# A fused mixer layer: the first two row pairs in eight plain products, and VectorE's SBUF pairs issued as scalar_tensor_tensor

## The chip, the cores and the metric

One NeuronCore of a Trainium2 chip runs the whole layer in one launch. The engines are PE (TensorE: matmuls and, through an identity matrix, transposes), DVE (VectorE), ACT (ScalarE), POOL (GpSimd) and SP, whose queue issues every DMA here. Each engine takes its instructions strictly in order and waits on semaphores for the others. The metric is device time in microseconds; each time below is the median of three runs or that of the one profiled execution.

## The reference, cut to what matters

```python
h = layer_norm(x, ln_emb_g, ln_emb_b)                    # x: 4096 rows x 1024
a_val, a_gate, a_z, b_u, b_v, b_z = split(h @ w_in, 6)   # six parts of 512 columns
y_a = silu(layer_norm(depthwise_conv31(a_val * sigmoid(a_gate)))) * silu(a_z)
y_b = gelu(b_u) * (w_s_lower_triangular @ layer_norm(gelu(b_v)) + b_s) * silu(b_z)
h = layer_norm(2**0.25 * h + concat(y_a, y_b) @ w_out)
h = h + sigmoid(h @ w_ple_gate + b_ple_gate) * (p @ w_ple)
```

Everything is float32.

## The kernel before, in words

The matrix work is five units of the same form, (4096 x 1024) times (1024 x 1024): `a_val|a_gate`, `b_u|b_v`, `b_z|a_z`, `w_out` and `w_ple_gate`. Below they are units A to E. A unit walks over 16 pairs of row blocks, 256 rows each. Within a pair both factors are cut into 2 x 2 blocks of 512 (256 rows are two blocks of 128), and the pair is computed in seven block products instead of eight: `group` forms products 1 to 7 of sums of blocks. `rows_left` makes the row sums s1 to s4 of a pair, `first_operands` and `combos` make the weight sums. A product is exact to float32 through a split: each factor is a high part (fp32r) and a low rest, and `product` issues three matmuls (high x high, high x low, low x high) for each of four k slices, so 12 matmuls of 128x128 by 512 columns a product, and 84 a pair.

The left factors are rows: loaded (`load_x`), normalised (`h_rows`: statistics on DVE, a power and a bias on POOL, scaling on ACT, then a multiply and an add by the embedding's gain and shift `eb`), turned by PE in groups of four transposes into one of two spare PSUM banks (tag "S"), copied by ACT (`zq`), split (`left`: high part by ACT, rest by DVE or POOL) and written to `qD` in DRAM for units B and C. `split_weight` makes the high part of a weight on ACT and the rest on DVE, by TENSOR_TENSOR on two SBUF operands. The rows of pair 1 are finished by DVE, those of later pairs by POOL.

Unit A starts from nothing: `load_first` loads four weight blocks, `first_operands` builds the sums W5, W6, W7, W4 in place and splits seven operands before pair 0. `open_banks` writes zeros by matmul into banks A and D, because `group` adds products onto copies that lie there. Later units get their weights from DRAM (`load_operands`, seven reads of 1 MB in the last pair of the unit before).

The convolution runs in the background on DVE, in chains of SCALAR_TENSOR_TENSOR (`conv`), with one SBUF operand and one PSUM accumulator each. Its two row buffers have the tag "ca"; nothing uses them until pair 3 of unit A has been written out. A scheduler arranges the instructions of each engine when the program is built, so the order of code is not the order on an engine; `tc.issue_after` keeps a piece of background work behind a given instruction.

Of the kernel before, what the change touches and what calls it, by code (L numbers as in the profile page):

```python
# [16 lines left out]
P = 128  # L17
# [47 lines left out]
def hybrid_layer_kernel(  # L65
# [51 lines left out]
    def flat(t):  # L117
        return t.rearrange("p k x -> p (k x)")
# [89 lines left out]

    def first_operands(W, stg):
        b11, b12, b22, b21 = (stg[ij] for ij in ((0, 0), (0, 1), (1, 1), (1, 0)))  # L210

        def sub(dst, a, b):
            for c in range(2):
                cs = slice(2 * c, 2 * c + 2)
                tt(dst[:, cs], a[:, cs], b[:, cs], op=SUB)
# [12 lines left out]

    def left(src, eng):
# [15 lines left out]
    def rows_left(L, rows, keep=None):  # L245
# [7 lines left out]
        def turn(n, j, half):  # L253
            tp = sbank("tp")
            for kk in range(4):
                k = 4 * half + kk
                nc.tensor.transpose(  # L257
                    out=tp[:, kk * P : (kk + 1) * P], in_=rows[:, j, k * P : (k + 1) * P],
                    identity=ident,
                )  # L260
            if keep is not None:
                act(zq[:, n], tp, ID)
            return quad(tp)
# [39 lines left out]
        yield  # L303

    def product(ps, n, L, W, start):
        ah, al = L[n]
        wh, wl = W[n]
# [6 lines left out]
    def open_banks():  # L316

        z = atile("zero")
        nc.gpsimd.memset(z.bitcast(F32), 0.0)
        for tag in ("A", "D"):  # L320
            nc.tensor.matmul(pbank(tag, "seed"), lhsT=z[:, 0, :], rhs=flat(z), start=True, stop=True)

    anchor = []

# [99 lines left out]
    def unit(u, L, W, next_left, next_first, body, conv_quota, lag=0):  # L424


        for p in range(NP):
# [9 lines left out]
            def between(i):  # L437
                bg_x.step(2 if lag else 1)
                if i >= lag:
                    bg.step(3 if lag else 2)  # L440
                bg_post.step(2)
                if last and u + 1 < 5:
                    bg_w.step(2 if i == 5 else 1)
                else:
                    bg_w.step(1)
                if i in (2, 3):
                    with tc.issue_after(anchor[0].ins):
                        bg_conv.step(conv_quota)
# [11 lines left out]
    X = {}  # L460

    def load_x(p):
        X[p] = big([P, 2, D], "xr")
        for j in (1, 0):
            dma(X[p][:, j], x[(2 * p + j) * P : (2 * p + j + 1) * P, :])

    def first_rows():

        r = X[0]
        for j in (1, 0):  # L470
            mv = mvtile(1)
            moments([r[:, j, 0:C], r[:, j, C:]], mv[:, 0, :])
            nb = scale_bias(mv)
            act(r[:, j], r[:, j], ID, scale=mv[:, 0, 1:2], bias=nb[:, 0:1])
            for half in (0, 1):
                v = r[:, j, half * C : (half + 1) * C]
                tt(v, v, eb[:, 0, half * C : (half + 1) * C], op=MUL)
                tt(v, v, eb[:, 1, half * C : (half + 1) * C], op=ADD)
            dma(hT[0][j], r[:, j])

    def h_rows(p, eng):

        r = X[p]
        mv = mvtile(2)
        for j in (1, 0):
            moments([r[:, j, 0:C], r[:, j, C:]], mv[:, j, :])
        yield
        nb = scale_bias(mv)
        for j in (1, 0):
            act(r[:, j], r[:, j], ID, scale=mv[:, j, 1:2], bias=nb[:, j : j + 1])  # L490
            eng.tensor_tensor(r[:, j], r[:, j], eb[:, 0], op=MUL)
            eng.tensor_tensor(r[:, j], r[:, j], eb[:, 1], op=ADD)
            dma(hT[p][j], r[:, j])
            yield
# [3 lines left out]
    eb = broadcast(erow, 2, "eb")  # L498
    stg = load_first()
    first_rows()  # L500
    open_banks()
    L = {}
    for _ in rows_left(L, X.pop(0), qD[0]):
        pass
    first_operands(W, stg)
    dma(cw_sb, cw)
# [3 lines left out]
    dma(bs_sb, bsv)  # L510
    load_x(1)
    for _ in h_rows(1, nc.vector):
        pass

    def left_a(p, L):
        return rows_left(L, X.pop(p), qD[p])

# [22 lines left out]
    def body_a(p, L, W, between):  # L540
        if p + 2 < NP:
            load_x(p + 2)
            bg_x.add(h_rows(p + 2, nc.gpsimd))
        if p == 3:
            bg_w.add(combos(1))
        c12, c22 = utile([P, C], "c12"), utile([P, C], "c22")
        pa, pd = group(L, W, None, c12, c22, between)
        for ps, c in ((pa, c12), (pd, c22)):
            act(c, c, AF.Sigmoid)
            tt(c, ps, c, op=MUL)  # L550
# [17 lines left out]
    act(wsx[:, 0], wsf, ID)  # L568
    tt(wsx[:, 1], wsf, wsx[:, 0].bitcast(F32), op=SUB)
    V = {}  # L570
# [17 lines left out]
    def body_b(p, L, W, between):  # L588
# [6 lines left out]
        def norm_v(j, v):  # L595
# [5 lines left out]
            act(v, v, ID, scale=mv[:, 0, 1:2], bias=nb[:, 0:1])  # L601
            tt(v, v, sgb[0][:, 0], op=MUL)
            tt(v, v, sgb[1][:, 0], op=ADD)
            act(V["h"][:, i], v, ID)
# [92 lines left out]
    def left_y(p, L):  # L697
        return rows_left(L, Y.pop(p))

# [61 lines left out]
    def left_z(p, L):  # L761
        return rows_left(L, Z[p])

# [125 lines left out]
```

## Time and profile before

| | us |
|---|---|
| median of three runs (lowest, highest) | 1899.16 (1896.24, 1899.81) |
| the profiled execution's own time | 1898.2 |
| its span, first to last instruction | 1896.5 |
| PE busy in the span | 1804.0 (95%) |
| DVE busy | 1413.6 (75%) |
| POOL busy | 1269.9 (67%) |
| ACT busy | 892.4 (47%) |

PE's busy time counts matmuls that overlap, so it says where PE stands still rather than how fast it goes. Of the 92 us in which PE is idle, 33 lie in the first 60 us; most of the rest lies where one unit ends and the next begins.

### The profile page before, as it was taken

The page shows a single profiled execution, that of the slowest core. Times are in us where ns is not written, and L with a number is a line of the kernel's source. Part 1 is how long each engine was busy: PE and PEld are TensorE (multiplying, and loading weights), DVE is VectorE, ACT ScalarE, POOL GpSimd, SP SyncE. Part 2 cuts the span into 40 slices and gives each one's busy share as a digit, 9 for nine tenths or more (in the row PEclk, how much of TensorE's full clock was granted, in tenths as well). Part 3 has the DMA queues.
Part 4 walks back from the last instruction along what each step waited for, and adds up shares of the span by engine and source line. Part 5 has one row for each costly group of instructions (what it writes and reads, how often), then busy time and mean ns, then how long its engine had stood idle before and what let it go on. Part 6 is the DMA issues. An engine that isn't in the chain of part 4 may idle for free. (4 is left out here: it accounts for less than half of the span.)

```text
span 1896.5 us, 24392 instructions
## 1 busy us (share of the span) xinstructions
PE 1804.0 (95%) x8322; PEld 1470.9 (78%) x8322; DVE 1413.6 (75%) x2176; ACT 892.4 (47%) x1438; POOL 1269.9 (67%) x1015
## 2 busy tenths in 40 slices
PE   4799999999999999999999899999999999999999
PEld 3687788877788887788888677787887787888887
DVE  8637877797787778978787998887558856665654
ACT  4655555565455555544444634445555422332222
POOL 2878987458777676588668568757676856655541
PEclk9899999999999999999999889999999999999999
DMA  6579776586734445898666758745555322222311
GB/s 239 195 236 359 248 235 206 194 287 211 239 124 147 139 142 173 302 358 298 211 198 227 272 186 284 242 150 191 197 189 220 119 95 78 89 90 95 100 54 52
DMA packets 184940, 363.62 MB, mean 192 GB/s; under 512 B 49648, under 2 KB 74224, under 8 KB 177136
## 3 DMA queue, kind: packets, MB, share of 16 engines
q1 hardware_dynamic: 184816, 362.07, 55.3%
q8 instruction: 66, 1.08, 0.2%
q14 instruction: 58, 0.48, 0.1%
HBM read 211.02 MB, written 150.99 MB: 191 GB/s over the span
## 5 line engine op out<-in xcount | busy, mean ns | idle before, releaser
L232 POOL TENSOR_TENSOR alo<-s,ahi 128x512 fp32r<-128x512 f32 x192 | 262.8, 1382 | 260.7 <-ACT ahi L231 252.9
L312 PE MATMUL pb<-whi,ahi 128*128 128x512 f32 x960 | 385.9, 402 | 18.3 <-ACT pa L330 5.2
L313 PE MATMUL pb<-wlo,ahi 128*128 128x512 f32 x960 | 378.4, 394 | 1.6 <-DVE wlo L173 1.6
L314 PE MATMUL pb<-whi,alo 128*128 128x512 f32 x960 | 378.4, 394 | 0.1
L312 PE MATMUL pe<-whi,ahi 128*128 128x512 f32 x640 | 258.9, 405 | 19.6 <-ACT ahi L231 8.5
L314 PE MATMUL pe<-whi,alo 128*128 128x512 f32 x640 | 256.6, 401 | 2.1 <-POOL alo L232 2.1
L313 PE MATMUL pe<-wlo,ahi 128*128 128x512 f32 x640 | 254.6, 398 | 4.2 <-DVE wlo L173 4.2
L312 PEld LDWEIGHTS pb<-whi,ahi 128*128 128x128 f32 x960 | 182.3, 190 | 63.6 <-ACT pa L330 8.8
L314 PEld LDWEIGHTS pb<-whi,alo 128*128 128x128 f32 x960 | 182.1, 190 | 39.5 <-POOL alo L232 0.6
L313 PEld LDWEIGHTS pb<-wlo,ahi 128*128 128x128 f32 x960 | 182.7, 190 | 38.4 <-DVE wlo L173 2.6
L232 POOL TENSOR_TENSOR alo<-qa,ahi 128x512 fp32r<-128x512 f32 x128 | 171.2, 1353 | 48.1 <-ACT ahi L231 47.8
L231 ACT ACTIVATE ahi<-s 128x512 fp32r<-128x512 f32 x192 | 119.7, 629 | 138.9 <-DVE s L284 54.6
L386 DVE SCALAR_TENSOR_TENSOR acc<-ca,cs_sb,acc 128x512 f32<-128x512 f32 x240 | 180.1, 750 | 4.3
L395 DVE SCALAR_TENSOR_TENSOR acc<-ca,cw_sb,acc 128x512 f32<-128x512 f32 x240 | 179.0, 746 | 0.1
L392 DVE SCALAR_TENSOR_TENSOR acc<-zy,cw_sb,acc 128x512 f32<-128x512 f32 x224 | 166.8, 745 | 1.2 <-POOL zy L378 0.4
L312 PEld LDWEIGHTS pe<-whi,ahi 128*128 128x128 f32 x640 | 122.7, 192 | 47.1 <-ACT ahi L231 10.3
L232 POOL TENSOR_TENSOR alo<-qb,ahi 128x512 fp32r<-128x512 f32 x96 | 126.8, 1329 | 39.2 <-ACT ahi L231 38.2
L313 PEld LDWEIGHTS pe<-wlo,ahi 128*128 128x128 f32 x640 | 122.6, 191 | 30.4 <-DVE wlo L173 6.5
L232 DVE TENSOR_TENSOR alo<-tp,ahi 128x512 fp32r<-128x512 f32 x144 | 98.2, 683 | 62.9 <-ACT ahi L231 60.5
L314 PEld LDWEIGHTS pe<-whi,alo 128*128 128x128 f32 x640 | 122.3, 191 | 27.8 <-POOL alo L232 3.3
L312 PE MATMUL pd<-whi,ahi 128*128 128x512 f32 x320 | 129.4, 404 | 4.4 <-ACT pd L330 3.2
L159 POOL TENSOR_TENSOR mv<-mv,nhalf 128x2 f32<-128x2 f32 (+1 forms) x81 | 55.2, 687 | 111.2 <-DVE mv L158 110.3
(151 smaller groups left out, 4006.7 us busy)
## 6 DMA issues: line engine op xcount, KB each, us to landing
qa<-qD SPq DMA_DIRECT2D x32, 1024.0 KB, 6.5
twD<-bq SPq DMA_DIRECT2D x112, 256.0 KB, 5.7
wst<-twD SPq DMA_DIRECT2D x28, 1024.0 KB, 6.9
qb<-qD SPq DMA_DIRECT2D x32, 768.0 KB, 6.8
xr<-in_x SPq DMA_DIRECT2D x32, 512.0 KB, 5.4
hT<-xr SPq DMA_DIRECT2D x32, 512.0 KB, 3.8
qD<-s SPq DMA_DIRECT2D x64, 256.0 KB, 2.9
bq<-in_wq SPq DMA_DIRECT2D x64, 256.0 KB, 5.2
```

The source lines that it names most:

```text
L159: ptt(mv[:, :, 1], mv[:, :, 1], nhalf[:, 0:n], op=ALU.pow)
L231: act(hi, src, ID)
L232: eng.tensor_tensor(lo, src, hi.bitcast(F32), op=SUB)
L312: nc.tensor.matmul(ps, lhsT=ah[:, k, :], rhs=wh[:, k, :], start=start and k == 0, stop=False, **kw)
L313: nc.tensor.matmul(ps, lhsT=ah[:, k, :], rhs=wl[:, k, :], start=False, stop=False, **kw)
L314: nc.tensor.matmul(ps, lhsT=al[:, k, :], rhs=wh[:, k, :], start=False, stop=k == 3, **kw)
L386: stt(even, src, w, even, op0=MUL, op1=ADD)
L392: stt(dst, src, cw_sb[:, ct, 2 * k + 1 : 2 * k + 2], odd if k else even, op0=MUL, op1=ADD)
L395: stt(src if k == NE - 1 else even, src, cw_sb[:, ct, 2 * k : 2 * k + 1], even, op0=MUL, op1=ADD,)
```

## The change

It has four parts. (1) `ss` is a new helper: VectorE's operations on two SBUF tensors become SCALAR_TENSOR_TENSOR, (a x 1.0) op b, flattened to two dimensions, at ten places; operations with a PSUM operand stay TENSOR_TENSOR. (2) Pairs 0 and 1 of unit A use `first_left` and `first_group`: eight plain products of the unsummed blocks, 96 matmuls, with no copies between banks; `open_banks` goes, and each bank is opened by its first product. The row sums are still made, but only to be written to `qD` (s2 on POOL), and they are not split. The sigmoid reads PSUM. (3) The weight sums and their splits (`rest_operands`, W5, W6, W7, W4) move from ahead of pair 0 to behind pair 1's last row sum (`made`). (4) The rows of pairs 1 and 2 are loaded into the convolution's two "ca" buffers, and row block 0 goes ahead of block 1 in pairs 0 and 1.

```diff
+    def ss(out, a, b, op):
+        return stt(out, a, 1.0, b, op0=MUL, op1=op)
...
             act(hi[:, cs], stg[:, cs], ID)
-            tt(lo[:, cs], stg[:, cs], hi[:, cs].bitcast(F32), op=SUB)
+            ss(flat(lo[:, cs]), flat(stg[:, cs]), flat(hi[:, cs].bitcast(F32)), op=SUB)
...
-    def first_operands(W, stg):
+    def rest_operands(W, stg):
...
-        W[1] = split_weight(b11)
         sub(b11, b12, b11)
         W[5] = split_weight(b11)
-        W[3] = split_weight(b22)
         sub(b12, b22, b12)
         sub(b22, b22, b11)
         W[6] = split_weight(b22)
+        yield
         W[7] = split_weight(b12)
-        W[2] = split_weight(b21)
         sub(b21, b21, b22)
+        yield
         W[4] = split_weight(b21)
...
+    def first_left(L, rows, keep):
+        zq = big([P, 4, C], "zq")
+        def turn(n, j, half):
...
+            act(zq[:, n], tp, ID)
+            L[j, half] = left(quad(tp), nc.vector)
+            return tp
...
+        t22 = turn(3, 1, 1)
+        s1 = utile([P, C], "s1")
+        tt(s1, t22, zq[:, 2], op=ADD)
+        t12 = turn(1, 0, 1)
+        s2 = utile([P, C], "s2")
+        ptt(s2, s1, zq[:, 0], op=SUB)
+        yield
+        s4 = utile([P, C], "s4")
+        made[:] = [tt(s4, t12, s2, op=SUB)]
...
+    def first_group(L, W, to12, to22, between):
+        anchor.clear()
+        pa, pd, pb, pe = (pbank(tag, "first") for tag in "ADBE")
+        for i, (ps, l, w, start) in enumerate((
+            (pa, (0, 0), 1, True), (pd, (1, 0), 1, True),
+            (pb, (0, 0), 12, True), (pe, (1, 0), 12, True),
+            (pb, (0, 1), 3, False), (pe, (1, 1), 3, False),
+            (pa, (0, 1), 2, False), (pd, (1, 1), 2, False),
+        )):
+            product(ps, l, L, W, start, w)
+            if i == 4:
+                act(to12, pb, AF.Sigmoid)
...
     def load_x(p):
-        X[p] = big([P, 2, D], "xr")
-        for j in (1, 0):
-            dma(X[p][:, j], x[(2 * p + j) * P : (2 * p + j + 1) * P, :])
+        if p in (1, 2):
+            X[p] = [row_tile("xr") for j in range(2)]
...
+        for j in order(p):
+            dma(X[p][j], x[(2 * p + j) * P : (2 * p + j + 1) * P, :])
...
-            bg_x.add(h_rows(p + 2, nc.gpsimd))
+            bg_x.add(h_rows(p + 2, ptt))
...
+        if p == 1:
+            rest = rest_operands(W, stg)
+            with tc.issue_after(made[0].ins):
+                next(rest)
```

On PE, where the work opens, the program before has the three row groups of transposes and then products of sums (tp is a transposed row group, pe and pb are PSUM banks, ahi and alo the split rows, whi and wlo the split weights):

```order
L321 MATMUL seed<-zero 128x512 x2
L257 MATMUL tp<-ident,xr 128x128 x12
L312 MATMUL pe<-whi,ahi 128x512
L313 MATMUL pe<-wlo,ahi 128x512
L314 MATMUL pe<-whi,alo 128x512
```

The changed program has one row group, and then products of plain blocks into the banks named "first":

```order
L318 MATMUL tp<-ident,xr 128x128 x4
L355 MATMUL first<-whi,ahi 128x512
L356 MATMUL first<-wlo,ahi 128x512
L355 MATMUL first<-whi,ahi 128x512
L318 MATMUL tp<-ident,xr 128x128 x8
L357 MATMUL first<-whi,alo 128x512
```

The first product moved ahead of two of the row groups, and the zero matmuls are gone. On PE between pair 1 and pair 2 (ta are transposes of unit A's output, xr the rows of pairs 2 and 3, pb and pe the banks of pair 2) the changed program reads:

```order
L357 MATMUL first<-whi,alo 128x512
L262 MATMUL tp<-ident,xr 128x128 x8
L593 MATMUL ta<-ident,c_340 128x128 x4
L593 MATMUL ta<-ident,c_341 128x128 x4
L262 MATMUL tp<-ident,xr 128x128 x12
L355 MATMUL pb<-whi,ahi 128x512
```

All seven groups of transposes stand behind pair 1's last matmul and ahead of pair 2's first one; before, such groups stand between the products of the pair ahead. On POOL in the opening the program before has the splits of pair 0's row sums (alo), the powers and biases of the row statistics (mv, nb), and pair 2's rows (xr):

```order
L232 TENSOR_TENSOR alo<-s_244,ahi 128x512
L232 TENSOR_TENSOR alo<-s_265,ahi 128x512
L232 TENSOR_TENSOR alo<-s_272,ahi 128x512
L232 TENSOR_TENSOR alo<-s_285,ahi 128x512
L159 TENSOR_TENSOR mv<-mv,nhalf 128x2
L161 TENSOR_SCALAR nb<-mv 128x1 x2
L159 TENSOR_TENSOR mv<-mv,nhalf 128x2
L161 TENSOR_SCALAR nb<-mv 128x1 x2
L491 TENSOR_TENSOR xr<-xr,eb 128x1024 x2
L492 TENSOR_TENSOR xr<-xr,eb 128x1024 x2
```

The changed program has there (xr_336 and xr_337 are the two row blocks of pair 2, xr_524 those of pair 3):

```order
L340 TENSOR_TENSOR s2_433<-s1_421,zq_367 128x512
L163 TENSOR_TENSOR mv_358<-mv_358,nhalf_71 128x2
L165 TENSOR_SCALAR nb_402<-mv_358 128x1 x2
L163 TENSOR_TENSOR mv_563<-mv_563,nhalf_71 128x2
L165 TENSOR_SCALAR nb_625<-mv_563 128x1 x2
L556 TENSOR_TENSOR xr_336<-xr_336,eb_180 128x1024
L556 TENSOR_TENSOR xr_337<-xr_337,eb_180 128x1024
L557 TENSOR_TENSOR xr_336<-xr_336,eb_180 128x1024
L556 TENSOR_TENSOR xr_524<-xr_524,eb_180 128x1024 x2
L557 TENSOR_TENSOR xr_337<-xr_337,eb_180 128x1024
L557 TENSOR_TENSOR xr_524<-xr_524,eb_180 128x1024 x2
```

The splits are gone, and the add on xr_337, whose transposes come first on PE, is the sixth of eight operations on rows. On DVE in the changed program, between pair 2's row statistics (st_359, st_363, gathered in mv_358) stand the weight sums (wst) and splits (wlo):

```order
L152 BN_AGGR mv_358<-st_359 128x2
L151 BN_STATS st_363<-xr_336 128x6 x2
L151 BN_STATS st_564<-xr_524 128x6
L93 SCALAR_TENSOR_TENSOR wst_186<-wst_189,wst_186 128x1024
L151 BN_STATS st_564<-xr_524 128x6
L151 BN_STATS st_568<-xr_524 128x6 x2
L93 SCALAR_TENSOR_TENSOR wlo_532<-wst_183,whi_531 128x1024
L93 SCALAR_TENSOR_TENSOR wst_186<-wst_189,wst_186 128x1024
L93 SCALAR_TENSOR_TENSOR wlo_532<-wst_183,whi_531 128x1024
L152 BN_AGGR mv_358<-st_363 128x2
```

Before, these sums and splits stand ahead of pair 1's rows.

## Rows read from the trace of the kernel before

**Rows 1.** Stretches: length, busy time of each engine, granted clock, DMA share, GB/s.
```profile
core 0: us, PE busy (x) PEld busy (x) DVE busy (x) ACT busy (x) POOL busy (x), PEclk, DMA share, GB/s
0.00:60.00 60.00, 26.85 (x82) 18.58 (x83) 51.44 (x65) 28.82 (x34) 21.94 (x26) 0.89 0.54 199
...
400.00:450.00 50.00, 43.83 (x182) 34.32 (x181) 44.39 (x56) 29.25 (x45) 31.13 (x26) 0.93 0.64 219
725.00:775.00 50.00, 42.45 (x184) 31.81 (x183) 42.30 (x59) 32.27 (x46) 24.25 (x22) 1.00 0.70 240
1050.00:1100.00 50.00, 40.19 (x156) 31.49 (x155) 49.87 (x54) 26.39 (x37) 19.63 (x14) 0.83 0.73 262
...
1440.00:1525.00 85.00, 75.75 (x325) 59.13 (x326) 67.62 (x76) 37.83 (x53) 61.32 (x32) 0.96 0.44 158
```

**Rows 2.** Instructions in order of time, PE: start, duration, idle before and releaser.
```profile
12.23 1.09 PE L257 MATMUL tp<-ident,xr 128*128 128x128 f32 x4 [9.47 <-ACT whi L172]
59.21 2.94 PE L257 MATMUL tp<-ident,xr 128*128 128x128 f32 x12 [9.41 <-DVE xr L492]
70.56 0.39 PE L314 MATMUL pd<-whi,alo 128*128 128x512 f32 x1
70.78 0.39 PE L314 MATMUL pe<-whi,alo 128*128 128x512 f32 x1
95.12 0.39 PE L314 MATMUL pd<-whi,alo 128*128 128x512 f32 x1
116.97 0.39 PE L314 MATMUL pd<-whi,alo 128*128 128x512 f32 x1
```

**Rows 3.** In order of time, DVE and POOL in the opening.
```profile
20.19 4.61 POOL L232 TENSOR_TENSOR alo<-s,ahi 128x512 fp32r<-128x512 f32 x1 [11.07 <-ACT ahi L231]
55.31 5.96 POOL L491 TENSOR_TENSOR xr<-xr,eb 128x1024 f32<-128x1024 f32 x2 [4.01 <-ACT xr L490]
58.99 3.37 DVE L173 TENSOR_TENSOR wlo<-wst,whi 128x1024 fp32r<-128x1024 f32 x1
```

**Rows 4.** DVE's groups by shape, whole span: busy, mean ns, idle before.
```profile
L392 DVE SCALAR_TENSOR_TENSOR acc<-zy,cw_sb,acc 128x512 f32<-128x512 f32 x224 | 166.8, 745 | 1.2 <-POOL zy L378 0.4
L173 DVE TENSOR_TENSOR wlo<-wst,whi 128x1024 fp32r<-128x1024 f32 x70 | 116.5, 1682 | 7.5 <-ACT whi L172 6.7 <-PE pb L314 0.8
L350 DVE TENSOR_TENSOR c<-pe,u 128x512 f32<-128x512 f32 x32 | 22.0, 689 | 19.7 <-PE pe L314 13.0 <-ACT u L330 4.5 <-POOL mv L159 1.2
```

**Rows 5.** Single lines: shortest, median, longest ns of one, first and last start.
```profile
L392 DVE SCALAR_TENSOR_TENSOR acc<-zy,cw_sb,acc x224: 698/747/757, 185.9 to 1314.8; 128x512 f32<-128x512 f32 x112
L158 DVE TENSOR_SCALAR mv<-mv x81: 113/151/2094, 7.2 to 1461.1; 128x2 f32<-128x2 f32 x47, 128x1 f32<-128x1 f32 x34
L173 DVE TENSOR_TENSOR wlo<-wst,whi x70: 1164/1216/7503, 13.8 to 1475.1; 128x1024 fp32r<-128x1024 f32 x70
L491 POOL TENSOR_TENSOR xr<-xr,eb x28: 2367/2406/3335, 55.3 to 350.1; 128x1024 f32<-128x1024 f32 x28
```

**Rows 6.** Opening 130 us, groups by shape, and DMA issues of 0:60 (KB, us to landing).
```profile
L147 DVE BATCH_NORM_STATS2 st<-xr 128x6 f32<-128x512 f32 x24 | 15.2, 672 | 10.9 <-DMA xr<-in_x 10.9
L215 DVE TENSOR_TENSOR wst<-wst 128x1024 f32<-128x1024 f32 x8 | 9.4, 1207 | 0.0
L490 ACT ACTIVATE xr<-xr,nb,mv 128x1024 f32<-128x1024 f32 x10 | 12.0, 1232 | 11.5 <-POOL nb L161 11.5
...
xr<-in_x SPq DMA_DIRECT2D x8, 512.0 KB, 5.4
```

**Rows 7.** Weight splits on DVE in 400:450, 725:775, 1050:1100, 1440:1525, in this order.
```profile
L173 DVE TENSOR_TENSOR wlo<-wst,whi 128x1024 fp32r<-128x1024 f32 x10 | 16.4, 1652 | 0.0
L173 DVE TENSOR_TENSOR wlo<-wst,whi 128x1024 fp32r<-128x1024 f32 x13 | 18.5, 1437 | 2.2 <-ACT whi L172 1.4 <-PE pb L314 0.8
L173 DVE TENSOR_TENSOR wlo<-wst,whi 128x1024 fp32r<-128x1024 f32 x14 | 27.0, 1943 | 0.0
L173 DVE TENSOR_TENSOR wlo<-wst,whi 128x1024 fp32r<-128x1024 f32 x12 | 22.5, 1903 | 0.0
```

More of the change, by code (lines that the diff above doesn't have):

```diff
@@ L257, in turn @@
                 nc.tensor.transpose(
-                    out=tp[:, kk * P : (kk + 1) * P], in_=rows[:, j, k * P : (k + 1) * P],
+                    out=tp[:, kk * P : (kk + 1) * P], in_=rows[j][:, k * P : (k + 1) * P],
                     identity=ident,
@@ L303, in rows_left, with put, product @@
         yield
-    def product(ps, n, L, W, start):
+    def first_left(L, rows, keep):
+        zq = big([P, 4, C], "zq")
+        def turn(n, j, half):
+            tp = sbank("tp")
+            for kk in range(4):
+                k = 4 * half + kk
+                nc.tensor.transpose(
+                    out=tp[:, kk * P : (kk + 1) * P], in_=rows[j][:, k * P : (k + 1) * P],
+                    identity=ident,
+                )
+            act(zq[:, n], tp, ID)
+            L[j, half] = left(quad(tp), nc.vector)
+            return tp
+        def put(n, src):
+            dma(keep[:, ORDER.index(n)], src)
+        turn(0, 0, 0)
+        yield
+        t21 = turn(2, 1, 0)
+        s3 = utile([P, C], "s3")
+        tt(s3, zq[:, 0], t21, op=SUB)
+        yield
+        t22 = turn(3, 1, 1)
[4 more added lines that the diff above has]
+        ptt(s2, s1, zq[:, 0], op=SUB)
+        yield
+        s4 = utile([P, C], "s4")
+        made[:] = [tt(s4, t12, s2, op=SUB)]
+        for n, src in ((7, s3), (5, s1), (6, s2), (3, s4), (1, zq[:, 0]), (2, zq[:, 1]), (4, zq[:, 3])):
+            put(n, src)
+        yield
+    def product(ps, n, L, W, start, w=None):
         ah, al = L[n]
-        wh, wl = W[n]
+        wh, wl = W[n if w is None else w]
         kw = dict(skip_group_check=True)
@@ L314, in product @@
             nc.tensor.matmul(ps, lhsT=al[:, k, :], rhs=wh[:, k, :], start=False, stop=k == 3, **kw)
[L316 to L323, printed above, removed]
+    anchor, made = [], []
+    def first_group(L, W, to12, to22, between):
[10 more added lines that the diff above has]
+                act(to12, pb, AF.Sigmoid)
+            elif i == 5:
+                act(to22, pe, AF.Sigmoid)
+            if i < 6:
+                between(i)
+        return pa, pd
     def group(L, W, add, to12, to22, between, scale=None):
@@ L445, in between @@
                     bg_w.step(1)
[L446 removed]
+                if i in (2, 3) and anchor:
                     with tc.issue_after(anchor[0].ins):
@@ L460, in hybrid_layer_kernel, with row_tile, order, h_rows @@
     X = {}
+    def row_tile(name):
+        return pool.tile([P, D], F32, tag="ca", name=name, bufs=2)
+    def order(p):
+        return (0, 1) if p < 2 else (1, 0)
     def load_x(p):
[L463 to L465 removed]
+        if p in (1, 2):
+            X[p] = [row_tile("xr") for j in range(2)]
+        else:
+            t = big([P, 2, D], "xr")
+            X[p] = [t[:, j] for j in range(2)]
+        for j in order(p):
+            dma(X[p][j], x[(2 * p + j) * P : (2 * p + j + 1) * P, :])
     def first_rows():
         r = X[0]
[L470 removed]
+        for j in (0, 1):
             mv = mvtile(1)
[L472 removed]
+            moments([r[j][:, 0:C], r[j][:, C:]], mv[:, 0, :])
             nb = scale_bias(mv)
[L474 removed]
+            act(r[j], r[j], ID, scale=mv[:, 0, 1:2], bias=nb[:, 0:1])
             for half in (0, 1):
[L476 to L481, printed above, removed]
+                v = r[j][:, half * C : (half + 1) * C]
+                ss(v, v, eb[:, 0, half * C : (half + 1) * C], op=MUL)
+                ss(v, v, eb[:, 1, half * C : (half + 1) * C], op=ADD)
+            dma(hT[0][j], r[j])
+    def h_rows(p, both):
         r = X[p]
         mv = mvtile(2)
[L485 to L486 removed]
+        for j in order(p):
+            moments([r[j][:, 0:C], r[j][:, C:]], mv[:, j, :])
         yield
         nb = scale_bias(mv)
[L489 to L493, printed above, removed]
+        for j in order(p):
+            act(r[j], r[j], ID, scale=mv[:, j, 1:2], bias=nb[:, j : j + 1])
+            both(r[j], r[j], eb[:, 0], op=MUL)
+            both(r[j], r[j], eb[:, 1], op=ADD)
+            dma(hT[p][j], r[j])
             yield
@@ L546, in body_a, with between_1 @@
         c12, c22 = utile([P, C], "c12"), utile([P, C], "c22")
-        pa, pd = group(L, W, None, c12, c22, between)
+        if p == 1:
+            rest = rest_operands(W, stg)
+            with tc.issue_after(made[0].ins):
+                next(rest)
+            def between_1(i):
+                if i in (1, 4):
+                    with tc.issue_after(made[0].ins):
+                        next(rest)
+                between(i)
+            pa, pd = first_group(L, W, c12, c22, between_1)
+        elif p == 0:
+            pa, pd = first_group(L, W, c12, c22, between)
+        else:
+            pa, pd = group(L, W, None, c12, c22, between)
         for ps, c in ((pa, c12), (pd, c22)):
-            act(c, c, AF.Sigmoid)
+            if p > 1:
+                act(c, c, AF.Sigmoid)
             tt(c, ps, c, op=MUL)
```

34 lines of the change are left out of this document (18 added, 16 removed).

## The prediction

> **What bounds the kernel now.** I read the page's busy times first: PE works 1804.0 of 1896.5 us, so a change can win only what PE stands idle (92 us), and it loses whatever it adds to PE. The view of stretches says where the idle time lies [rows 1]. In the first 60 us PE is busy 26.85, so 33.15 are idle. The four stretches in which one unit ends and the next begins have 6.2, 7.5, 9.8 and 9.25 us (length less PE busy), 32.8 together. In 1050:1100 DVE is busy 49.87 of 50 us and the granted clock of PE is 0.83, between its two levels: PE waits for DVE there, and restarts slowly.
>
> Next the order in time on PE [rows 2]. Its first transposes start at 12.23, pair 1's at 59.21, after 9.41 us of waiting for DVE's last row operation. Matmuls of 128x512 follow each other by 0.22 us (70.56 to 70.78). Pair 1's last product is reached at 95.12, pair 2's at 116.97: 21.85 us for a pair of 84 matmuls with six groups of transposes among them. Taking 0.46 for a group leaves 19.1, or 0.2275 a matmul, which I use below.
>
> Last, what makes DVE and POOL late. In the opening a POOL subtraction of 128x512 takes 4.61 us, and a DVE split of 128x1024 takes 3.37 [rows 3]. Over the span that split (L173) has a shortest time of 1164, a median of 1216 and a longest of 7503 ns [rows 5] with a mean of 1682 [rows 4], while the weight sums of the same shape have 1207 [rows 6]. The work is the same, so the rest is waiting inside the instruction, and it appears where both engines work on SBUF operands. DVE's operations with one operand in PSUM show none: L350 has a mean of 689 [rows 4], the convolution's SCALAR_TENSOR_TENSOR (L392) 698 to 757 [rows 5].
>
> **Pairs 0 and 1, the gain.** Eight products of 12 matmuls instead of seven: 2 x 12 x 0.2275 = 5.5 us more on PE. In exchange pair 0 waits for three split weights fewer and for no row sum. Before, the first product needs W5, a sum; after, it needs one plain weight and one row group, both of which are there at the same time as before (transposes at 12.23 [rows 2], then a copy, two split steps, and the first weight's split). I put its steady part at about 19; then 8 x 12 x 0.2275 = 21.8 gives the end of pair 0 at 41. Pair 1's transposes need the two spare banks, and its first product the banks that the sigmoid frees on ACT behind copies and high parts: I take 7 us of gap, so 48 + 21.8 = 70. Before it was 95.3. That is 25 us earlier, with the 5.5 paid.
>
> **Pair 2's rows, which take most of it back.** They are loaded into "ca", and those buffers hold pair 1's rows until its transposes have read them, at about 45. The load takes 5.4 [rows 6], so they stand in SBUF at 50. Then, in this order:
> - DVE: eight statistics of 0.672 [rows 6] for two pairs, and between them, by the new order, eight operations of 1.2 on weights and some smaller ones: 5.4 + 9.6 + 2 = 17, so the last aggregate is at 67. Were no weight work between them it would be about 57.
> - POOL's power and bias, and ACT's scaling at 1.23 [rows 6]: about 3, so 70.
> - POOL: the row block whose transposes come first is finished by the sixth of eight 128x1024 operations. At the median of 2406 ns [rows 5], 6 x 2.41 = 14.4, so 84 to 85. With waiting for DVE as two of them show in the opening (5.96 for two instead of 4.81 [rows 3]) and with five DVE operations of 1.2 among them, 6 more: about 90.
>
> PE is idle from 70 to 84, or to 90. Then seven groups of transposes go through two spare banks ahead of pair 2's first product, each pair of groups waiting for copies and splits. For these I take 10 us (bounds 4, the transposes alone, and 14, where DVE's statistics of the next load of 5.4 us stand in the way). So pair 2 starts at 84 + 10 = 94. Up to the state of the row at 116.97 it has 84 x 0.2275 + 6 x 0.46 = 21.9 of its own, 2.7 for the product of pair 3 that is done by then, and 2 for the slow clock after so long a wait: 94 + 26.6 = 120.6 against 117.2. The opening costs about 3 us (0 to 8) if DVE and POOL do not wait for each other, and 9 (5 to 14) if they do.
>
> **The new form on DVE.** No instruction of before is a SCALAR_TENSOR_TENSOR on two SBUF tensors. The nearest rows are the 128x512 one with a PSUM operand (745 mean) and the TENSOR_TENSOR (689) [rows 4]: 8% more at the top. On 128x1024 that is 1.21 to 1.30, so 0 to 1 us in a transition of 10 to 14 splits. The other bound is a form that runs at half that rate; only a longer instruction, 2.4, would show it.
>
> What the form does to the waiting is the main unknown. Two readings fit the rows. By one, the wait belongs to TENSOR_TENSOR: the one SCALAR_TENSOR_TENSOR in the trace, 224 of them over 1100 us beside a busy POOL, never exceeds 757 ns [rows 5]. By the other, it belongs to the second SBUF operand: that same instruction has one operand in PSUM, and so has L350. Against a pure count of operands stands L158, one-input and 128x2 at most, with a median of 151 and a longest of 2094 ns [rows 5]: an instruction with one SBUF tensor waits too, so the form of the instruction matters.
>
> The Trainium skill, "SBUF — State Buffer", section "Who interferes with whom", speaks against this change: by it a VectorE instruction with two SBUF inputs contends with a GpSimd one that reads SBUF, since its second input comes through the shared read interface. By that rule the new form waits as the old one did; the same section lets one-input operations enter modes that contend, with which L158 agrees. No row of before can decide it for the new form.
>
> If the wait goes, each transition gains its splits' excess over 1.207, as far as PE is idle there [rows 1, 7]: 10 x 0.445 = 4.4 of 6.2; 13 x 0.23 = 3.0 of 7.5; 14 x 0.736 = 10.3, capped at 9.8; 12 x 0.696 = 8.4 of 9.25. Sum 25.6, taken as 25. The low bound is 10 (PE waits for loads or ACT next); the high one is the whole idle time of the four stretches, 32.8.
>
> **Rivals.**
> - A, the forecast: the new form does not wait. +3 - 25 = -22, so 1898.2 - 22 = 1876 against the profiled execution.
> - B, the other side: the new form waits as the old one. Nothing is won at the transitions (the same instructions, the same order but for details), and the opening costs 9: 1907 (1902 to 1912). Place: POOL's operations on pair 2's rows between 70 and 90, behind DVE's weight sums. It decides as soon as the transitions gain less than the opening loses. For it: the PSUM operand in every instruction that never waits.
> - C, the opening pays in full: pair 2's rows are ready by about 70 because the scheduler's order lets them through sooner than I count. Then of the 25 us some 22 stay and with 25 at the transitions 1850 results. Against it: eight POOL operations at 2.41 are 19.2 us by themselves, behind a load that can't start before 45.
> - D, the new form is slow: with 2.4 instead of 1.2 for a split, 1050:1100, where DVE has no free time, grows by up to 14 x 0.46 = 6.4 over its mean of 1.943, the others by up to 7 to 15 each less what is hidden: 1915 to 1930.
>
> **How the numbers follow.** Chances: A 0.55, B 0.33, C 0.05, D 0.07. A and B are near each other since one row speaks on each side; I lean to A as the row with a single tensor that waits shows that operand count isn't the whole rule. The profiled execution (1898.2) lies 1 below the median of runs (1899.16), so 1876 becomes 1877. A by itself has 1862 to 1892: from +3 - 33 = -30 with a little of C, to +8 - 10 = -2 with some of the low end left out. B reaches 1912. The range that leaves out no more than 2 in 10 is 1861 to 1909: it cuts C, most of D, and the upper half of B's tail. What a measurement of this kernel can tell from no change is about 0.2%, 3.8 us. Faster by more than that: 0.50 of A and all of C, 0.55. Within it: 0.05 of A's upper end and 0.06 of B's lower end, 0.11. Slower: the other 0.27 of B, and D, 0.34.
>
> **What the profile of the changed kernel would show.** Right: 128x1024 SCALAR_TENSOR_TENSOR splits near 1.2 us with no tail, also beside POOL, and POOL's 128x512 subtractions in a narrow band; pair 0's last product near 41 and pair 1's near 70; PE idle for over 10 us from there, released by POOL's add on the rows; pair 2's last product at 117 to 125; 1050:1100 and 1440:1525 with less idle on PE. B would show splits with means of 1.6 to 1.9 again and idle times at the transitions as before. D would show a shortest split well over 1.3. The sum is wrong if another engine's wait takes over at a transition whose splits have become short, or if the gap behind pair 1 is short.

## The result

The changed kernel takes 1910.45 us (median of 19 runs, 1901.74 to 1921.13) where the kernel before took 1898.19 (19 runs): a ratio of 1.0059, 95% interval 1.0047 to 1.0072. It is slower by 11 to 12 us. The forecast was 1877, and 1910.45 also lies above the range. It is rival B, "the new form waits as the old one", that came true: it gave 1907, with 9 us lost in the opening and nothing won where the units end.

PE of the changed kernel in order of time (start, duration, idle before and what ended it), to be laid beside [rows 2]:

```profile
41.48 0.48 PE L357 MATMUL first<-whi,alo 128*128 128x512 f32 x1
...
49.51 0.79 PE L355 MATMUL first<-whi,ahi 128*128 128x512 f32 x1 [3.08 <-ACT c L373]
...
73.97 0.39 PE L357 MATMUL first<-whi,alo 128*128 128x512 f32 x1
...
88.67 1.97 PE L262 MATMUL tp<-ident,xr 128*128 128x128 f32 x8 [14.31 <-POOL xr L557]
...
100.90 0.78 PE L355 MATMUL pb<-whi,ahi 128*128 128x512 f32 x1
...
126.48 0.39 PE L357 MATMUL pd<-whi,alo 128*128 128x512 f32 x1
```

Pairs 0 and 1 are done at 74.2 instead of 95.3. Then PE stands idle for 14.31 us until POOL has finished pair 2's rows, and another 12.2 us pass until that pair's first product. Pair 2's last product comes at 126.48 instead of 116.97: 9.5 us late. POOL shows the rows on their way:

```profile
65.52 1.62 POOL L163 TENSOR_TENSOR mv<-mv,nhalf 128x2 f32<-128x2 f32 x1 [17.32 <-DVE mv L162]
67.24 3.99 POOL L165 TENSOR_SCALAR nb<-mv 128x1 f32<-128x1 f32 x2
71.19 1.68 POOL L163 TENSOR_TENSOR mv<-mv,nhalf 128x2 f32<-128x2 f32 x1
72.97 0.84 POOL L165 TENSOR_SCALAR nb<-mv 128x1 f32<-128x1 f32 x2
73.78 4.66 POOL L556 TENSOR_TENSOR xr<-xr,eb 128x1024 f32<-128x1024 f32 x2
78.40 3.32 POOL L557 TENSOR_TENSOR xr<-xr,eb 128x1024 f32<-128x1024 f32 x1
81.69 4.63 POOL L556 TENSOR_TENSOR xr<-xr,eb 128x1024 f32<-128x1024 f32 x2
86.28 6.96 POOL L557 TENSOR_TENSOR xr<-xr,eb 128x1024 f32<-128x1024 f32 x3
```

Six operations on numbers of 128x2 and 128x1 take 8.1 us, beside DVE's weight sums and splits; only then do the row operations begin, and the sixth ends at 88.6. Three such small operations at 31.27, with DVE not at work on SBUF pairs, take 1.2 us together, so some 5.7 of the 8.1 are waiting.

The stretches at the unit ends, as in [rows 1] (length, then PE, PEld, DVE, ACT, POOL busy, granted clock), and the weight splits in them, as in [rows 7]:

```profile
400.00:450.00 50.00, 43.80 (x181) 34.03 (x180) 45.29 (x53) 32.01 (x48) 30.21 (x24) 0.93 0.76 258
...
725.00:775.00 50.00, 42.76 (x188) 32.73 (x187) 42.87 (x66) 29.82 (x45) 29.25 (x25) 1.00 0.65 227
...
1050.00:1100.00 50.00, 42.23 (x186) 33.39 (x184) 49.52 (x57) 30.16 (x43) 26.45 (x19) 0.93 0.80 291
...
1440.00:1525.00 85.00, 76.73 (x337) 60.70 (x336) 67.54 (x76) 41.26 (x57) 63.66 (x33) 0.96 0.45 161
```

```profile
L93 DVE SCALAR_TENSOR_TENSOR wlo<-wst,whi 128x1024 fp32r<-128x1024 f32 x12 | 20.4, 1716 | 0.5 <-ACT whi L176 0.5
L93 DVE SCALAR_TENSOR_TENSOR wlo<-wst,whi 128x1024 fp32r<-128x1024 f32 x10 | 14.3, 1439 | 0.6 <-ACT whi L176 0.5
L93 DVE SCALAR_TENSOR_TENSOR wlo<-wst,whi 128x1024 fp32r<-128x1024 f32 x14 | 22.7, 1640 | 0.0
L93 DVE SCALAR_TENSOR_TENSOR wlo<-wst,whi 128x1024 fp32r<-128x1024 f32 x14 | 23.5, 1697 | 1.7 <-ACT whi L176 1.7
```

PE's idle time there is 6.2 + 7.2 + 7.8 + 8.3 = 29.5 us, where it was 32.8. The splits have means of 1.44 to 1.72 us under their new name; over the span they have a shortest of 1166 and a median of 1216 ns, as before [rows 5], and a longest of 3432. They still wait.

Where the 11.5 us between the two spans arise is seen at three points of each trace. Unit A's last transposes of its output start 5.7 us late (425.3, before 419.6), so unit A wins back 3.8 of the 9.5. Unit E's first gate product starts 5.2 us late (1484.9, before 1479.7), so units B to D are level in this execution. Its last one starts 11.6 us late (1902.7, before 1891.1). The rest of the loss lies in unit E, in a place of which the prediction does not speak. These are two single executions: in a second profile of the changed kernel (below) pair 2's last product is 11.1 us late, unit A's last transposes 6.9, and units B to D take 5.6 us more than before, so a difference of 5 or 6 us in units B to D can be one of single executions.

### The profile page after: what moved, and what is told of

Same layout as the page of the kernel before. It is cut to its first block, busy times and chain, and to the rows that moved or that the text cites. A ratio compares the mean times of both kernels' runs of the same rounds, so it can differ in the third digit from the quotient of the medians.

```text
span 1908.0 us, 24394 instructions
## 1 busy us (share of the span) xinstructions
PE 1807.0 (95%) x8344; PEld 1475.8 (77%) x8344; DVE 1403.6 (74%) x2174; ACT 888.1 (47%) x1426; POOL 1265.6 (66%) x1008
## 4 chain that ended last, share of the span: by engine, by line
PE 59%; DVE 12%; POOL 11%; DMA 10%; issue 4%; ACT 3%; SPq 1%; POOLq 0%; DVEq 0%; ACTq 0%
PE pb L355 7%; PE pb L356 7%; PE pb L357 7%; PE pe L355 5%; PE pe L357 5%; PE pe L356 5%; POOL alo L237 3%; PE tp L262 3%; PE pa L356 2%; PE pa L355 2%; DVE wlo L93 2%; PE pa L357 2%; PE pd L355 2%; PE pd L357 2%; PE pd L356 2%
## 5 line engine op out<-in xcount | busy, mean ns | idle before, releaser
L237 POOL TENSOR_TENSOR alo<-s,ahi 128x512 fp32r<-128x512 f32 x184 | 246.6, 1352 | 252.1 <-ACT ahi L236 244.3
L355 PE MATMUL pb<-whi,ahi 128*128 128x512 f32 x936 | 376.4, 402 | 25.2 <-DVE pa L387 8.5
L356 PE MATMUL pb<-wlo,ahi 128*128 128x512 f32 x936 | 368.6, 394 | 3.0 <-DVE wlo L93 3.0
L357 PE MATMUL pb<-whi,alo 128*128 128x512 f32 x936 | 369.2, 394 | 0.0
L355 PE MATMUL pe<-whi,ahi 128*128 128x512 f32 x624 | 250.0, 401 | 9.0 <-DVE v L405 3.8
L357 PE MATMUL pe<-whi,alo 128*128 128x512 f32 x624 | 247.9, 397 | 4.0 <-POOL alo L237 4.0
L356 PE MATMUL pe<-wlo,ahi 128*128 128x512 f32 x624 | 246.6, 395 | 1.3 <-DVE wlo L93 1.2
L355 PEld LDWEIGHTS pb<-whi,ahi 128*128 128x128 f32 x936 | 177.6, 190 | 69.9 <-issue 10.5
L356 PEld LDWEIGHTS pb<-wlo,ahi 128*128 128x128 f32 x936 | 177.6, 190 | 38.8 <-DVE wlo L93 4.4
L236 ACT ACTIVATE ahi<-s 128x512 fp32r<-128x512 f32 x184 | 114.4, 629 | 139.8 <-DVE s L279 63.9
L237 DVE TENSOR_TENSOR alo<-tp,ahi 128x512 fp32r<-128x512 f32 x146 | 99.3, 683 | 74.2 <-ACT ahi L236 74.0
```

The lines of the kernel that those rows point to most:

```text
L236: act(hi, src, ID)
L237: eng.tensor_tensor(lo, src, hi.bitcast(F32), op=SUB)
```

## The experiments

Ratios are to the kernel before on the same chip in the same rounds, with 95% intervals.

**The form by itself on chip.** Each stretch is 16 times one of these, on one engine or on both (`o`, `a`, `b` are 128x1024 in SBUF, `e`, `c`, `d` 128x512 in SBUF, `acc` in PSUM):

```diff
+    def v_tt():
+        tt(o, a, b, op=SUB)
+    def v_stt():
+        stt(o, a, 1.0, b, op0=MUL, op1=SUB)
+    def v_acc():
+        stt(acc, a[:, 0:C], 0.5, acc, op0=MUL, op1=SUB)
...
+    def p_tt():
+        ptt(e, c, d, op=SUB)
```

> Leaves out the whole layer: twelve stretches of 16 equal instructions on VectorE and GpSimd, alone and beside each other, on SBUF tensors (128x1024 on VectorE, 128x512 on GpSimd). Theory (the second SBUF operand makes the wait): beside GpSimd's TENSOR_TENSOR, VectorE's SCALAR_TENSOR_TENSOR and TENSOR_TENSOR on two SBUF tensors both stretch alike, from 1.2 us alone to 1.6 or more, and GpSimd's from 1.28 to 1.6 or more; with one operand in PSUM, and for BN_STATS, both keep their time alone. Rival (the form TENSOR_TENSOR makes it): SCALAR_TENSOR_TENSOR stays at 1.2 and GpSimd beside it at 1.28, only TENSOR_TENSOR stretches.

DVE in order of time; the duration is that of all 16, and GpSimd's rows follow:

```profile
7.55 20.12 DVE L105 TENSOR_TENSOR o<-a,b 128x1024 f32<-128x1024 f32 x16
...
49.91 35.20 DVE L105 TENSOR_TENSOR o<-a,b 128x1024 f32<-128x1024 f32 x16
...
85.65 20.12 DVE L108 SCALAR_TENSOR_TENSOR o<-a,b 128x1024 f32<-128x1024 f32 x16
...
106.31 35.20 DVE L108 SCALAR_TENSOR_TENSOR o<-a,b 128x1024 f32<-128x1024 f32 x16
...
142.05 11.63 DVE L111 SCALAR_TENSOR_TENSOR acc<-a,acc 128x512 f32<-128x512 f32 x16
...
163.77 11.62 DVE L114 TENSOR_SCALAR o<-a 128x1024 f32<-128x1024 f32 x16
...
175.92 26.67 DVE L114 TENSOR_SCALAR o<-a 128x1024 f32<-128x1024 f32 x16
```

```profile
28.07 21.36 POOL L120 TENSOR_TENSOR e<-c,d 128x512 f32<-128x512 f32 x16
...
106.17 34.26 POOL L120 TENSOR_TENSOR e<-c,d 128x512 f32<-128x512 f32 x16
...
141.91 21.39 POOL L120 TENSOR_TENSOR e<-c,d 128x512 f32<-128x512 f32 x16
```

This settles the question on which the forecast hung. The two forms on two SBUF tensors agree to the last digit: 20.12 us alone, 35.20 beside GpSimd, whose own 16 grow from 21.36 to 34.26. With one operand in PSUM GpSimd keeps its time (21.39), and DVE's 16 of 128x512 take 11.63, where 16 of that shape on two SBUF tensors take 11.59 alone in the next run. For these two forms the wait goes with the SBUF operands, not with the name. The rule that the prediction draws on, from the Trainium skill, "SBUF — State Buffer", section "Who interferes with whom", holds here for SCALAR_TENSOR_TENSOR as for TENSOR_TENSOR.

**One tensor, and small instructions.** The prediction took L158, with one operand and still a long wait [rows 5], for a sign that the form decides.

```diff
+    def v_str():
+        nc.vector.tensor_scalar(
+            o.rearrange("p (k x) -> p x k", k=2), a.rearrange("p (k x) -> p x k", k=2),
+            0.5, 1.0, op0=MUL, op1=ADD,
+        )
...
+    def p_small():
+        ptt(e[:, 0:2], c[:, 2:4], d[:, 2:4], op=SUB)
```

> Leaves out the whole layer: more stretches of 16 equal instructions. First the same one-tensor TENSOR_SCALAR of 128x1024, but walked across (512x2, so that neighbours in memory are not neighbours in the order). Theory (the one-tensor form waits only where it runs at the doubled rate that it showed alone): walked across it takes 1.2 us alone and the same beside GpSimd. Rival (every TENSOR_SCALAR waits): it stretches beside GpSimd as the straight one did (0.73 to 1.66 us apart). The 128x2 one waits for GpSimd's instruction to end in both cases, above 1 us each. The SCALAR_TENSOR_TENSOR of 128x512 stretches from 0.69 to about 1.4 to 2.0, with its second operand in PSUM not at all. GpSimd's TENSOR_TENSOR of 128x2, 0.3 or less alone, takes about 1.2 beside VectorE's 128x1024.

DVE, and then GpSimd's 128x2 alone (15 of them) and beside DVE's 128x1024:

```profile
7.23 20.15 DVE L117 TENSOR_SCALAR o<-a 128x1024 f32<-128x1024 f32 x16
...
27.92 31.79 DVE L117 TENSOR_SCALAR o<-a 128x1024 f32<-128x1024 f32 x16
...
60.13 10.73 DVE L123 TENSOR_SCALAR o<-a 128x2 f32<-128x2 f32 x16
...
94.15 26.68 DVE L126 SCALAR_TENSOR_TENSOR o<-a,b 128x512 f32<-128x512 f32 x16
...
121.36 11.51 DVE L129 SCALAR_TENSOR_TENSOR o<-a,acc 128x512 f32<-128x512 f32 x16
```

```profile
143.26 4.02 POOL L132 TENSOR_TENSOR e<-c,d 128x2 f32<-128x2 f32 x15
147.55 20.13 POOL L132 TENSOR_TENSOR e<-c,d 128x2 f32<-128x2 f32 x16 [0.27 <-DVE a L148]
```

The rival of that expectation won: TENSOR_SCALAR with one SBUF tensor waits in either walk (1.26 us each alone, 1.99 beside GpSimd). The 128x2 one takes 0.67 us a piece beside GpSimd, less than the 1 us expected; it was not run alone. So L158 was no sign against the operands: SBUF-only instructions of one and of two tensors can both wait. (BN_STATS, also on one SBUF tensor, did not: 11.62 us for 16 beside GpSimd, which stayed at 21.40.) GpSimd's 128x2 goes from 0.27 to 1.26 us, the time of one DVE instruction each. The 8.1 us for six at 65.52 to 73.78 above are of the same size.

**The form alone in the kernel before.** Ten lines like this one:

```diff
-            tt(lo[:, cs], stg[:, cs], hi[:, cs].bitcast(F32), op=SUB)
+            ss(flat(lo[:, cs]), flat(stg[:, cs]), flat(hi[:, cs].bitcast(F32)), op=SUB)
```

> The kernel before with VectorE's ten places changed to scalar_tensor_tensor, and nothing else. Theory (the new form waits as the old one, all of the loss is in the opening): 1898, within 3 us of the kernel before; the mean of the weight splits stays above 1.5 us. Rival (the form shortens the waits by what the splits' mean shows after the change, 1532 against 1682 ns, and the opening costs more than it seems): 1890 to 1893, with PE's idle time at the unit ends shorter by 5 us or more.

1897.43 us, ratio 0.9997 (0.9984 to 1.0011): no difference.

```profile
1050.00:1100.00 50.00, 40.34 (x155) 31.27 (x154) 49.71 (x51) 27.46 (x39) 21.32 (x15) 0.83 0.74 261
```

DVE is as full and PE as idle as in [rows 1]; the 14 splits there have a mean of 1949 ns, against 1943 [rows 7].

**The opening alone.** The changed kernel with `ss` issuing TENSOR_TENSOR:

```diff
-        return stt(out, a, 1.0, b, op0=MUL, op1=op)
+        return tt(out, a, b, op=op)
```

> The changed kernel with those ten places as tensor_tensor, the order of instructions on PE and GpSimd unchanged. Theory: the time of the changed kernel, 1907 to 1913; pair 2's last product 8 to 11 us later than in the kernel before, and nothing of it won back later. Rival (the form wins 5 us or more): 1915 to 1918.

1913.15 us, ratio 1.0073 (1.0051 to 1.0094), on the upper edge of what was expected; its interval and the changed kernel's (1.0047 to 1.0072) overlap. Pair 2's last product comes 11.2 us late (128.16), and unit E's gate products take 421.3 us from the first to the last (before 411.4). Together with the run before, the loss belongs to the opening and to the order of instructions that came with it, and not to the form.

**Pair 2's rows, from two sides.** First (sums_later) the weight sums tied behind pair 2's statistics, then (rows2_by_dve) pair 2's multiply and add on DVE, then (rows2_first) both, with the sums behind the last add. `seen[2]` is the last of pair 2's statistics in the first, its last add in the third:

```diff
-            with tc.issue_after(made[0].ins):
+            with tc.issue_after(seen[2].ins):
...
-            bg_x.add(h_rows(p + 2, ptt))
+            bg_x.add(h_rows(p + 2, ss if p == 0 else ptt))
```

> The changed kernel with the sums and splits of the other weights tied behind pair 2's row statistics instead of pair 1's last row sum, so that on VectorE no weight operation stands between those statistics, and on GpSimd the add on the rows whose transposes come first is fourth of eight row operations instead of sixth. Theory (pair 2's rows, late through VectorE's weight work and GpSimd's row operations, set PE's idle time behind pair 1): the idle time of 14.3 us before pair 2's first transposes falls to 2 to 7, and the kernel takes 1898 to 1903. Rival (what is late is the load into the convolution's buffers, or the transposes and splits behind it): it falls by less than 4, and the time stays above 1906.

> The changed kernel with pair 2's multiply and add by the embedding's gain and shift on VectorE instead of GpSimd; the weight sums stay where the change put them. Theory (what is late is GpSimd's sixth row operation, 15 us behind its start): the idle time before pair 2's first transposes falls from 14.3 to 3 to 7, and the time to 1898 to 1903. Rival (VectorE's weight sums hold the rows in either case, since they also stand ahead of the multiply there): it stays above 10, and 1907 or more.

> The changed kernel with both: pair 2's multiply and add on VectorE, and all sums and splits of the other weights behind the last of these adds. Theory (with pair 2's rows in time the opening pays, since pairs 0 and 1 end 22 us earlier than before): rows finished before pair 1 ends, no idle time over 3 us ahead of pair 2's first transposes; pair 2's last product at 108 to 114 instead of 126.5 (before the change 117), and 1889 to 1895. Rival (the weights' sums become the wait that ends last, with four high parts and splits of the sums behind them on ACT and VectorE): pair 2's last product not ahead of 117, and 1898 or more.

The first gave 1902.71 us, ratio 1.0020 (1.0007 to 1.0033), the second 1902.61, 1.0023 (1.0005 to 1.0041), the third 1904.24, 1.0026 (1.0010 to 1.0042). PE ahead of pair 2's first transposes, in that order:

```profile
83.19 1.97 PE L262 MATMUL tp<-ident,xr 128*128 128x128 f32 x8 [9.38 <-POOL xr L557]
```

```profile
83.39 1.94 PE L262 MATMUL tp<-ident,xr 128*128 128x128 f32 x8 [10.05 <-DVE xr L93]
```

```profile
74.10 1.35 PE L262 MATMUL tp<-ident,xr 128*128 128x128 f32 x8 [3.18 <-DVE xr L93]
...
87.21 1.12 PE L593 MATMUL ta<-ident,c 128*128 128x128 f32 x4 [6.78 <-ACT at L597]
```

Either edit alone takes 4 to 5 us off the 14.3, less than I wrote (the second stays at its rival's 10, though not at its 1907), and about 6 off pair 2's last product (120.6 and 120.2), so these rows did set the end. With both, pair 2's first transposes stand ahead of pair 1's last matmuls on PE, which waits there 3.18 us for the rows, and pair 1's last product comes at 79.6 instead of 74.0. Pair 2's last product comes at 123.9: the rival came true. DVE and ACT show why:

```profile
63.89 6.77 DVE L93 SCALAR_TENSOR_TENSOR wst<-wst 128x1024 f32<-128x1024 f32 x2
70.58 3.37 DVE L93 SCALAR_TENSOR_TENSOR xr<-xr,eb 128x1024 f32<-128x1024 f32 x1
73.88 3.38 DVE L93 SCALAR_TENSOR_TENSOR wst<-wst 128x1024 f32<-128x1024 f32 x1
...
81.83 4.84 ACT L176 ACTIVATE whi<-wst 128x1024 fp32r<-128x1024 f32 x5 [5.74 <-DVE wst L93]
```

Weight sums of 1.2 us take 3.4 beside POOL's operations on pair 3's rows. The high parts of the sums come late on ACT, and the copy (L597) for which PE waits 6.78 us stands behind them there.

**The sums on GpSimd, in time.** GpSimd is busy 6.9 of the changed kernel's first 60 us. Here it makes the weight sums (four subtractions in two halves each) as soon as pair 1's rows are done, and pair 2's multiply and add are on DVE as in rows2_by_dve; in a further run pair 4's statistics are tied behind pair 2's last split.

```diff
+    first = nc.gpsimd.tensor_copy(mark, X[1][1][:, D - 1 : D])
+    with tc.issue_after(first.ins):
+        rest_sums(stg)
```

> The changed kernel with the eight subtractions of the weight sums on GpSimd, from the moment that pair 1's rows are finished (a copy of one column of them makes GpSimd wait for that), the splits of the sums still on VectorE behind pair 1's last row sum, and pair 2's multiply and add on VectorE. Theory (pairs 0 and 1 really end 22 us earlier, and only rows or weights that come late take it back): both stand ready at about 70, when pair 1 ends; pair 2's last product at 102 to 110 (126.5 after the change, 117 before), and 1882 to 1891, faster than either kernel. Rival (the loss only moves again, to GpSimd's sums, which stretch beside VectorE's splits, or to the two spare banks): pair 2's last product at 115 or later, and 1896 or more.

> The kernel of the run sums_on_gpsimd with pair 4's row statistics tied behind pair 2's last split on VectorE; in that run they stood ahead of one of pair 2's splits and waited 6.0 us for a load, and PE stood idle for 7.2 us ahead of pair 2's first product. Theory (this wait ends last there): the idle time falls to under 3, pair 2's last product comes at 112 to 116 instead of 119.2, and the time to 1889 to 1894. Rival (another wait stands right behind it, on the two spare banks or ScalarE): pair 2's last product stays at 118 or later, and 1895 to 1898.

The first gave 1896.21 us, ratio 0.9977 (0.9964 to 0.9991): faster than the kernel before, but by 0.2% and not by the 0.4 to 0.9 that I expected. Pair 2's last product came at 119.2, since DVE waited 6.0 us for pair 4's load with one of pair 2's splits behind it: the rival's figures, for another reason than it named. The second removed that, pair 2's last product came at 114.9, ahead of the 116.97 of before and as expected, but the kernel took 1898.47, 1.0013 (1.0000 to 1.0026), not 1889 to 1894. Its opening is better by 4.3 us, but unit A ends only 1.1 earlier, unit D takes 409.1 us from the first to the last transpose of its rows where the other run takes 404.5, and the way from there to unit E's first gate product 88.3 instead of 85.5. In two profiles of the changed kernel the first of these two lengths differs by 2.8 us and the whole of units B to D by 6.1 (1059.6 and 1065.7), so one profile of each run can't tell this from chance; where the gain of the opening went stays open.

**What the waits are worth at the unit ends.** In the kernel before, ScalarE writes the low parts of the split weights as a scaled copy, so that DVE has no weight split at all; the values are left out. The second kernel adds two BN_STATS for each split on DVE.

```diff
-            tt(lo[:, cs], stg[:, cs], hi[:, cs].bitcast(F32), op=SUB)
+            act(lo[:, cs], stg[:, cs], ID, scale=2.0 ** -12)
```

> The kernel before, with the low parts of the split weights written by ScalarE as a scaled copy of the weight instead of by VectorE's subtraction: the 70 weight splits leave VectorE altogether, and with them their waits; the low parts' values are left out. Theory (the second step of the forecast: at the unit ends PE waits for VectorE's splits, whose waits are worth 25 us): 1865 to 1880, with PE's idle time at the four unit ends falling from 33 us to under 15. Rival (something else ends last there, the seven loads of 1 MB or ScalarE): 1888 or more, idle time over 25.

> As the run before, but VectorE keeps two BN_STATS of 128x512 on the same data for each split, 1.35 us that do not wait for GpSimd, so that only the waits are gone and not the work. Theory: 1868 to 1884, close to the run before, since it is the waits that count. Rival (VectorE's work itself is what counts at the unit ends): 10 us or more slower than the run before. Rival (neither): both at 1888 or more.

1901.62 us, 1.0007 (0.9993 to 1.0021), and 1917.40, 1.0083 (1.0057 to 1.0108). The stretches of the first:

```profile
400.00:450.00 50.00, 44.51 (x189) 36.31 (x190) 32.79 (x51) 36.84 (x57) 34.73 (x31) 0.93 0.60 195
...
725.00:775.00 50.00, 40.27 (x160) 31.25 (x159) 28.11 (x48) 40.65 (x55) 19.86 (x20) 0.90 0.72 246
...
1050.00:1100.00 50.00, 43.32 (x188) 34.74 (x187) 36.27 (x58) 40.44 (x54) 20.47 (x18) 0.93 0.76 275
...
1440.00:1525.00 85.00, 74.54 (x317) 59.33 (x316) 40.95 (x59) 47.99 (x65) 47.61 (x30) 0.92 0.43 152
```

DVE falls from 49.87 to 36.27 us in 1050:1100, and PE's idle time is 5.5 + 9.7 + 6.7 + 10.5 = 32.4, as before. In 725:775 PE now waits for ScalarE's copies between banks:

```profile
PE pd L312 <- ACT pd L330: 3.6, 1, 3.6
...
PE pb L312 <- ACT pa L330: 2.7, 2, 2.3
```

The theory failed in both; the rival's figures for the first (1888 or more, over 25 us idle) were met. The second is 15.8 us slower than the first, which meets the figure of its first rival too: 17.1 of the 21.6 us between their two spans lie between unit A's end and unit E's start, and whether at the unit ends was not followed up. The runs don't show what the waits alone are worth, since ScalarE took on a copy for each split, which also spoils the comparison of the second with the kernel before; they show that emptying DVE there is not enough to win the 25 us.

**The changed kernel again.** A second profile of it, with no edit.

> The changed kernel once more, for a second profile. Theory (the order of its loads in unit E costs some 6 us there, each time): the span from unit E's first to its last gate product is 416 to 420 us, as in its first profile (417.8; before 411.4), and PE waits 6 us or more for DVE's first copy of a pair between 50 and 300 us behind that start. Rival (chance of one execution): 411 to 413, and under 2 us.

1916.09 us. Unit E's gate products start from 1492.2 to 1909.1, 416.9 us (before 1479.7 to 1891.1, 411.4). PE's wait for DVE's first copy of a pair, between 50 and 300 us after unit E's first gate product (us in all, times, longest), in the kernel before, in the first profile of the changed kernel, and here:

```profile
PE pb L312 <- DVE pa L332: 1.1, 3, 0.7
...
PE pb L355 <- DVE pa L387: 7.2, 6, 2.9
...
PE pb L355 <- DVE pa L387: 7.8, 7, 3.1
```

It repeats. DVE in the first profile shows what stands ahead of that copy, the split of a block of p, which waits for ScalarE, which waits for the load of that block:

```profile
1612.08 0.69 DVE L93 SCALAR_TENSOR_TENSOR pl<-pf,ph 128x512 fp32r<-128x512 f32 x1 [5.00 <-ACT ph L876]
1612.69 0.69 DVE L387 TENSOR_TENSOR pa<-pb,gb 128x512 f32<-128x512 f32 x1
```

The run opening_alone, which has the same order of instructions in unit E, waits 6.5 us there; sums_later, which has another, 0.3. There are two such orders among the runs. In the kernel before, the form alone, sums_later, rows2_by_dve and sums_on_gpsimd, DVE, POOL and ACT have one and the same order in unit E, and the gate products take 411.4, 411.9, 412.2, 413.3 and 412.3 us. In the changed kernel (two profiles), opening_alone and rows2_first they have another, and it takes 417.8, 416.9, 421.3 and 414.6. So these 6 us belong to the second order. It is not an order of loads, as the expectation has it: from the second block of p on, SP issues its DMAs alike in all of them. In the pair shown, SP issued that load at 1608.26, when POOL had ended a split of a row sum (alo, 1606.48 to 1608.23); for such a split SP waits ahead of this load in every pair. Here a row operation of 2.39 us stands on POOL between the split before and this one, where in the kernel before this one follows at once. For the other pairs this was not followed up.

Unit E also holds part of what the edits to pair 2's rows won. By their ratios sums_later and rows2_by_dve are some 7 us faster than the changed kernel; their unit A ends 5.4 and 5.2 us earlier than in its first profile, and their unit E is 5.6 and 4.5 us shorter, which the edits did not aim at.

## Why the prediction was wrong

- **The step that failed** is the choice between the two readings of the wait: "I lean to A as the row with a single tensor that waits shows that operand count isn't the whole rule." The row was read rightly and proves nothing: one-tensor TENSOR_SCALAR waits (1.26 to 1.99 us), and so do both two-tensor forms (1.26 to 2.20). The new form waits as the old one did, so the 25 us of the second step were not there to win. The trace had the better evidence, hundreds of instructions with a PSUM operand that never wait; among them is L350, itself a TENSOR_TENSOR with a mean of 689 ns [rows 4], so the name alone could not be what waits. SCALAR_TENSOR_TENSOR with a PSUM operand kept to that when measured by itself.
- **"Each transition gains its splits' excess"** has no support either, though what the waits alone cost stayed open. With the splits moved from DVE to ScalarE PE was as idle as before at the unit ends (32.4 us, before 32.8); the 25 us were a sum of waits on one engine, and in 725:775 another engine's copies stood right behind them.
- **Pairs 0 and 1**: 41 for pair 0's end (41.5), 48 for pair 1's first product (49.5), 70 for its end (74.2). Of the 4 us, 1.5 are the later start and 2.8 the slow clock behind PE's wait: the first 14 matmuls follow each other by 0.43 us at a granted clock of 0.50 (the lower level, 1.2 GHz), the later ones by 0.227 at 1.00. The sum had that only for pair 2.
- **Pair 2's rows**: 70 for their start on POOL (73.8), 84 or 90 for the end of the sixth operation (88.6). The wait of 6 us was put on the row operations, which took 14.9 us for six (14.4 was the sum without waiting); it lay on the small ones ahead of them, 8.1 us where "POOL's power and bias, and ACT's scaling" had about 3 in all.
- **The opening by B**: 120.6 + 6 = 126.6 for pair 2's last product, 126.48 measured; 9 us lost, 9.5 measured (11.1 in the second profile). The mechanism is the one that B named; that the sum fits within 0.2 us is in part luck, as the rows' end (90, measured 88.6) and the way from there to the first product (10, measured 12.3) are off in opposite directions.
- **What no term had**: 3.8 us won back in unit A and 6.4 lost in unit E (4.2 and 5.5 in the second profile). They make 1910 out of B's 1907. The range ended at 1909, inside B's own 1902 to 1912, since B had only a third of the chance.

## What to carry to other kernels

Before an instruction is exchanged for one with another name, ask which memories its operands lie in: here two-tensor operations on SBUF waited for GpSimd under either name, and with one operand in PSUM they did not. Work saved on the bounding engine at the start pays only if the next item's whole chain (load, statistics, row operations, weights) is early by as much; each time one link was mended here, the next one held PE. A sum of waits on one engine is at best an upper bound of a gain and needs, for each wait, the name of what would be late next.

## What the hardware showed that was not expected

A VectorE instruction of 128x1024 and a GpSimd one of 128x512 that take 1.26 and 1.34 us alone take 2.20 and 2.14 beside each other, not far below the sum of 2.59, as if they mostly took turns. The smallest instructions lose the most for their size: beside the same 128x1024 of VectorE, GpSimd's operations on 128x2 rise from 0.27 to 1.26 us, by 0.99, those on 128x512 by 0.81. VectorE's 16 keep their time beside the small ones (20.12 us) and not beside the large ones (35.20). A TENSOR_SCALAR of one tensor takes 0.73 us for 128x1024 in straight order, 1.26 walked across, and both wait for GpSimd (1.67 and 1.99).
